# The head of the two MLPs of a decoder trunk: two weight pairs in step, operand sums on VectorE

## The chip, the cores and the metric

One core of a Trainium2 chip runs the whole kernel. The metric is device time in microseconds (us); of the kernel before, three runs took 2951.81, 2952.86 and 2962.06 us, the median is 2952.86 us. The engines have short names in the profile: PE is TensorE (matmul), PEld its weight loads, DVE is VectorE, ACT is ScalarE, POOL is GpSimd, SP is SyncE, which here issues all DMAs.

## The reference, cut to what matters

The trunk has two layers on 1040 tokens (16 meta tokens and 1024 of the input) with a model width of 1024. Each layer is attention with an output projection, and then an MLP with a squared ReLU:

```python
def rms_norm(x, g):
    y = xf * lax.rsqrt(jnp.mean(xf * xf, axis=-1, keepdims=True) + EPS)
    return y * g
def sq_relu_mlp(x, w1, w2):
    h = jax.nn.relu(x @ w1)
    return (h * h) @ w2
# per layer: h = h + attention(...) @ w_out ;  h = h + sq_relu_mlp(rms_norm(h, mlp_norm[i]), w1, w2)
```

w1 is 1024 x 4096 and w2 is 4096 x 1024. The attention parts are the same in both kernels and are not told here.

## The kernel before, in words

Everything is float32. A matrix operand is split into a high half, rounded to the matmul's short form, and a low half, the rest (`split`, L146: a copy on ScalarE, L141, and a subtract on VectorE, L148). A product takes three matmuls: high by high, high by low, low by high.

`mlp` (L902) does one layer's projection and MLP. Tokens are cut into two halves of H (520 in the first layer, 512 in the second), and both MLP matrices are multiplied by Winograd's form of Strassen's scheme: 2x2 blocks and seven products in place of eight. The blocks of the normed activations are x11 and x12 (half 0, channels 0 to 3 and 4 to 7 of 128) and x21 and x22 (half 1). The seven activation operands are A11 = x11, A12 = x12, S1 = x21 + x22, S2 = S1 - x11, S3 = x11 - x21, S4 = x12 - S2 and A22 = x22. A "pair" is 256 columns of the weights; 16 pairs make up w1 and 16 make up w2 (four for each block of 1024 rows), so a layer has 32 pairs of 7 products. A product (L994) is 24 matmuls of 128x260 in the first layer and 12 of 128x512 in the second. Its weight operand is b11, b12, b21, b22 or a sum of these (`w_sum` on GpSimd, L991), split in `w_op` (L965) into one of five buffers.

The order written in the code is: `project_out` (L818) multiplies the attention output by its weights, half 0 and then half 1, eight output tiles of 128 channels each. After each tile `out_evac` (L829) adds the result to the residual h and sums up the squares. `rnorm` (L845) makes 1/rms of a half in y; `normed` (L808) writes x11, x12 and their splits while half 1 is still being projected. After `rnorm(1)` comes the preparation (L936 to L955): for each of the four channel pairs j it makes x21 and x22 on VectorE, four sums on GpSimd and five splits. The pair loop starts at L1032. Its products use three PSUM accumulators: a (A11, S2, S3, A22 into the same one, read out in between), c (S1, then S4) and b (A12). The order is A11, S1, S2, then S4 of the pair before, S3, A12, A22. In w1's pairs the results are squared (`rsq`, or two activations), combined on GpSimd and stored in DRAM (`out`, L1006) in operand form; in w2's pairs they are added into h (`add`, L1014). When four pairs of a block are done, `refresh` (L1018) reads the next block's seven operands back from DRAM in 14 loads (L1027) through two buffers, and splits each.

Each engine runs its own list in order. The lists are drawn up when the kernel is built, by a scheduler that follows the written order as a priority and moves an instruction up where its estimate says that the engine would stand idle. Buffers that share a tag are reused when their last reader is done.

## Time and profile before

| | |
|---|---|
| median of three runs | 2952.86 us |
| the profiled execution, its span | 2952.59 us, 2950.8 us |
| busy: PE, DVE, ACT, POOL | 92%, 71%, 50%, 44% of the span |
| first layer: last projection matmul, first MLP product | 800.7 us, 804.2 us |
| second layer: last projection matmul, first MLP product | 2248.4 us, 2251.7 us |
| chain that ended last, by engine | PE 55%, DVE 21%, DMA 7%, POOL 6%, ACT 6%, issue 5% |

A row of the page or of the trace names the line, the engine and the operation, out<-in by the program's names without buffer numbers (`opa` holds A11 and A12, `opb` S1 and S2, `opc` S3, S4 and A22; `g` is a split weight operand, `t` a weight sum, `ac` a PSUM accumulator, `q` a squared result, `ld` a load buffer of `refresh`). In square brackets stands how long the engine had been idle and what ended that. Times count from the start of the span.

### The profile page before, as it was taken

Reading aid. Unit: us, or ns where it says so; the run is one execution under the profiler, and the core shown is the slowest. Engines: PE = TensorE matmul, PEld = TensorE weight load, DVE = VectorE, ACT = ScalarE, POOL = GpSimd, SP = SyncE. Lnnn points to the kernel's source line nnn. Section 1 sums busy time; section 2 is a strip of 40 time slices with the busy share of each in tenths; the row PEclk is TensorE's granted clock in tenths of the full one; section 3 lists DMA queues with packets and bytes.
Section 4 is the critical chain, followed back from the end, with each engine's and each line's share of the span. In section 5 each row is a group of like instructions: output and inputs, shape, how many; then the busy total and the mean of one; then the engine's idle time right before and its main releaser. Section 6 shows DMA issues by size and latency. Waiting matters only on the chain.

```text
span 2950.8 us, 45897 instructions
## 1 busy us (share of the span) xinstructions
PE 2708.3 (92%) x16698; PEld 2387.9 (81%) x16698; DVE 2092.0 (71%) x3826; ACT 1486.4 (50%) x2828; POOL 1311.3 (44%) x1210
## 2 busy tenths in 40 slices
PE   6889788999979999999988999999997999989999
PEld 6779655677969999999988888889775688867777
DVE  7999989684575456766766888888757655577774
ACT  5777577775333334333434666666743333333332
POOL 2356345431365555322334555555515555543231
PEclk9999779999979999999999999999998999999999
DMA  5312100002314445444411111111312344454442
GB/s 169 80 46 70 49 22 1 1 1 87 93 62 158 146 149 176 143 129 146 158 65 56 51 51 51 52 51 52 105 58 68 121 158 150 153 186 150 150 135 72
DMA packets 243154, 281.93 MB, mean 96 GB/s; under 512 B 22272, under 2 KB 183872, under 8 KB 242928
## 3 DMA queue, kind: packets, MB, share of 16 engines
q1 hardware_dynamic: 242928, 279.01, 30.7%
q8 instruction: 131, 2.15, 0.3%
q14 instruction: 95, 0.78, 0.1%
HBM read 192.42 MB, written 67.63 MB: 88 GB/s over the span
## 4 chain that ended last, share of the span: by engine, by line
PE 55%; DVE 21%; DMA 7%; POOL 6%; ACT 6%; issue 5%; SPq 0%; DVEq 0%; ACTq 0%; POOLq 0%
PE ac L999 32%; PE ps L186 6%; DMA ld<-rdr 5%; PE ps L199 5%; DVE sc L481 3%; PE ps L675 2%; PE ps L733 1%; PE ps L761 1%; PE ps L1322 1%; DVE sc L465 1%; POOL bp L1304 1%; PE ps L758 1%; PE ps L1344 1%; DVE g L148 1%; DVE opa L148 1%
## 5 line engine op out<-in xcount | busy, mean ns | idle before, releaser
L999 PE MATMUL ac<-opc,g 128*128 128x260 f32 (+1 forms) x3456 | 580.0, 324 | 33.5 <-ACT q L141 11.0
L999 PEld LDWEIGHTS ac<-opc,g 128*128 128x128 f32 x3456 | 504.9, 191 | 92.4 <-issue 14.2
L999 PE MATMUL ac<-opb,g 128*128 128x260 f32 (+1 forms) x2304 | 390.2, 325 | 50.8 <-ACT opb L141 35.2
L999 PEld LDWEIGHTS ac<-opb,g 128*128 128x128 f32 x2304 | 336.9, 191 | 94.6 <-ACT opb L141 41.0
L999 PE MATMUL ac<-opa,g 128*128 128x260 f32 (+1 forms) x2304 | 394.5, 324 | 1.6 <-ACT g L141 0.8
L999 PEld LDWEIGHTS ac<-opa,g 128*128 128x128 f32 x2304 | 340.5, 192 | 37.7 <-ACT g L141 1.1
L991 POOL TENSOR_TENSOR t<-rb,t 128x512 f32<-128x512 f32 x128 | 191.8, 1498 | 338.0 <-DMA rb<-in_mlp_w_dram 278.1
L148 DVE TENSOR_TENSOR g<-t,g 128x512 fp32r<-128x512 f32 x256 | 227.6, 889 | 133.5 <-ACT g L141 131.1
L141 ACT ACTIVATE g<-t 128x512 fp32r<-128x512 f32 x256 | 161.1, 629 | 264.2 <-PE ac L999 161.8
L199 PE MATMUL ps<-xhb,wh 128*128 128x256 f32 (+5 forms) x640 | 205.1, 320 | 5.9 <-DVE z L1151 2.7
L199 PE MATMUL ps<-xhb,wl 128*128 128x256 f32 (+5 forms) x640 | 196.8, 307 | 0.0
L199 PE MATMUL ps<-xlb,wh 128*128 128x256 f32 (+5 forms) x640 | 196.3, 307 | 0.0
L991 POOL TENSOR_TENSOR t<-ra 128x512 f32<-128x512 f32 x64 | 95.3, 1489 | 177.4 <-DVE g L148 172.2
L1304 POOL TENSOR_SCALAR bp<-bp,bnm 128x400 f32<-128x400 f32 (+7 forms) x128 | 106.4, 842 | 143.5 <-DVE bnm L1302 143.3
L148 DVE TENSOR_TENSOR g<-rb,g 128x512 fp32r<-128x512 f32 x128 | 113.4, 886 | 57.0 <-ACT g L141 56.9
L675 PE MATMUL ps<-ks,qs 128*128 128x512 f32 (+4 forms) x448 | 131.0, 395 | 21.1 <-DVE qs L606 13.7
L141 ACT ACTIVATE q<-ac 128x520 f32<-128x520 f32 (+1 forms) x96 | 57.7, 601 | 164.4 <-PE ac L999 162.0
L1344 PE MATMUL ps<-bth,bvs 128*128 128x512 f32 (+1 forms) x420 | 135.4, 396 | 3.9 <-DVE qb L1351 2.2
L141 ACT ACTIVATE bth<-ps 128x512 fp32r<-128x512 f32 (+3 forms) x224 | 111.5, 502 | 52.5 <-PE ps L1322 46.5
L199 PEld LDWEIGHTS ps<-xhb,wh 128*128 128x128 f32 x640 | 122.0, 191 | 17.3 <-DVE kr L292 5.1
L148 DVE TENSOR_TENSOR bth<-ps,bth 128x512 fp32r<-128x512 f32 (+3 forms) x210 | 119.6, 571 | 23.0 <-ACT bth L141 21.9
L141 ACT ACTIVATE wh<-wr 128x1024 fp32r<-128x1024 f32 (+1 forms) x84 | 87.3, 1039 | 96.3 <-PE ps L186 71.5
(364 smaller groups left out, 6702.1 us busy)
## 6 DMA issues: line engine op xcount, KB each, us to landing
ra<-in_mlp_w_dram SPq DMA_DIRECT2D x64, 512.0 KB, 3.9
rb<-in_mlp_w_dram SPq DMA_DIRECT2D x64, 512.0 KB, 4.2
ld<-rdr SPq DMA_DIRECT2D x56, 520.0 KB, 4.0
ld<-rdr SPq DMA_DIRECT2D x56, 512.0 KB, 4.3
rdr<-q SPq DMA_DIRECT2D x64, 260.0 KB, 2.1
rdr<-q SPq DMA_DIRECT2D x64, 256.0 KB, 2.2
rdr<-qs SPq DMA_DIRECT2D x48, 260.0 KB, 2.0
wr<-in_a_w_in_dram SPq DMA_DIRECT2D x24, 512.0 KB, 4.1
```

The lines of the kernel that those rows point to most:

```text
L141: nc.scalar.activation(dst, src, AF.Copy, scale=scale)
L148: (nc.gpsimd if pool else nc.vector).tensor_tensor(lo, src, f32(hi), OP.subtract)
L186: nc.tensor.matmul(o[0:n, 0:m], a[:, k, 0:n], b[:, k, s:s + m], start=(k == 0 and j == 0), stop=(k == NK - 1 and j == 2))
L199: nc.tensor.matmul(o[0:n, 0:m], a[:, k, 0:n], b[:, k, s:s + m], start=(k == 0 and j == 0), stop=(k == NK - 1 and j == 2))
L465: nc.vector.scalar_tensor_tensor(sb[:, s:s + m], tm[:, 0:m], wsg[:, b, h:h + 1], sb[:, s:s + m], OP.mult, OP.add)
L481: nc.vector.tensor_scalar(eqb[:, 0:L[b]], scs(b), th, None, op, OP.add, accum_out=dst[:, b:b + 1])
L675: nc.tensor.matmul(o, qs[:, h, :], kc, start=(v == 0), stop=(v == 1))
L733: nc.tensor.transpose(pt[:, j * n:j * n + n], pr[j][:, c0:c0 + P], ident)
L991: nc.gpsimd.tensor_tensor(t, a, c, OP.subtract)
L999: nc.tensor.matmul(t[:, i, 0:m], a[:, j, :], c[:, j, o:o + m], start=start and j == 0 and v == 0, stop=stop and j == 3 and v == 2, skip_gr ...
L1304: nc.gpsimd.tensor_scalar(pr[i], pr[i], nm[:, 3, i:i + 1], 0.0, OP.mult, OP.add)
L1344: nc.tensor.matmul(po[:, j0 * P:], v_kb, th[0:rows, v, j0 * P:], start=(kb == 0 and v == 0), stop=(kb == last and v == 1))
```

## The change

- `out_evac`, in half 1, also sums h times the norm's gain over the two channels of a pair into `st[2]`: a scaled copy on ScalarE for tiles 0 to 3, a multiply-add on VectorE for tiles 4 to 7.
- The preparation is cut up by operand. S1 is that sum times y; S2 = S1 - x11 and S4 = x12 - S2 are made in place; S3 is x22 - S2, with x22 made from h, gain and y. All of it is on VectorE, four channels at a time.
- Pairs 0 and 1 go in step: A11 and A12 of pair 0, then of pair 1; S1 is prepared, and its product is taken for both pairs; then S2 and S4, with both products for both pairs; then S3 and A22. Their weight sums are on VectorE.
- From pair 2 on a pair's order is A11, S1, S2, A12, S4, S3, A22, with S4 within its own pair. S3 and A22 follow one another on accumulator a.
- Accumulators are taken from a list of four that are free, in order of release. `refresh` has three load buffers in place of two; weight sums have three in place of four. The first layer's input tiles for the residual use `st[2]`.

The diff, cut (the removed loop and preparation are in the listing above):

```diff
@@ normed
-                dst = st[j][:, i, 0:H]
+                dst = st[i][:, j, 0:H]
...
@@ out_evac
+                    if half:
+                        us = st[2][:, mi % 4, 0:H]
+                        if mi < 4:
+                            copy(us, sl, gain[:, mi:mi + 1])
+                        else:
+                            nc.vector.scalar_tensor_tensor(us, sl, gain[:, mi:mi + 1], us, OP.mult, OP.add)
...
@@ project_out, x_transposed
-                resid(op)
+                resid(st[2].rearrange("p a b -> p (a b)"))
...
-            xt = op.tile([P, D], F32, tag="xt2", name=f"xt2{t}", bufs=2)
+            xt = spare[:, t % 2 * D:t % 2 * D + D]
...
@@ mlp
-            st = [sp.tile([P, 2, HMAX], F32, name=f"st{layer}{j}") for j in range(4)]
+            st = [sp.tile([P, 4, HMAX], F32, tag=f"st{layer}{j}", name=f"st{layer}{j}") for j in range(3)]
...
+                free, tag_of = [0, 1, 2, 3], {}
                 def accum():
                     n_acc[0] += 1
-                    return pm_.tile([P, 2, 512], F32, tag="acc", name=f"ac{layer}_{n_acc[0]}")
+                    t = pm_.tile([P, 2, 512], F32, tag=f"acc{free[0]}", name=f"ac{layer}_{n_acc[0]}")
+                    tag_of[id(t)] = t, free.pop(0)
+                    return t
+
+                def done(t):
+                    free.append(tag_of.pop(id(t))[1])
+                    return t
...
...
+
+                def prepare(*os):
+                    for o in os:
+                        for j in range(4):
+                            x1, x2, u = (st[i][:, j, 0:H] for i in range(3))
+                            if o == S1:
+                                nc.vector.tensor_tensor(u, u, y[:, b:b + H], OP.mult)
+                                src = u
+                            elif o == S2:
+                                nc.vector.tensor_tensor(x1, u, x1, OP.subtract)
+                                src = x1
+                            elif o == S4:
+                                nc.vector.tensor_tensor(x2, x2, x1, OP.subtract)
+                                src = x2
+                            elif o == S3:
+                                nc.vector.scalar_tensor_tensor(u, h[:, j + 4, b:b + H], gain[:, j + 4:j + 5], y[:, b:b + H],
+                                                               OP.mult, OP.mult)
+                                nc.vector.tensor_tensor(x1, u, x1, OP.subtract)
+                                src = x1
+                            else:
+                                src = u
+                            split(ops[o][0][:, j], ops[o][1][:, j], src)
                 q11 = ep.tile([P, 2, HMAX], F32, tag="sq", name=f"q11_{layer}")
-                q12 = sp.tile([P, 2, HMAX], F32, tag=f"st{layer}0", name=f"q12_{layer}")
-                q2 = sp.tile([P, 2, HMAX], F32, tag=f"st{layer}1", name=f"q2_{layer}")
-                qs = ep.tile([P, 2, HMAX], F32, tag="acc", name=f"qs_{layer}")
+                late = {}
...
-                    t = mp.tile([P, 4, P], F32, tag="wt", name=f"t{layer}_{n}_{i}", bufs=4)
-                    nc.gpsimd.tensor_tensor(t, a, c, OP.subtract)
+                    t = mp.tile([P, 4, P], F32, tag="wt", name=f"t{layer}_{n}_{i}", bufs=3)
+                    (nc.vector if n < 2 else nc.gpsimd).tensor_tensor(t, a, c, OP.subtract)
...
-                        ld = sp.tile([P, 2, HMAX], F32, tag=f"st{layer}{2 + i % 2}", name=f"ld{layer}_{i}")[:, :, 0:H]
+                        if "ld" not in late:
+                            late["ld"] = sp.tile([P, 4, HMAX], F32, tag=f"st{layer}2", name=f"ld{layer}")
+                        g, o2 = ((late["ld"], 0), (late["ld"], 2), (late["c"], 2))[i % 3]
+                        ld = g[:, o2:o2 + 2, 0:H]
...
@@ mlp: the new pair(n) and the new loop; the old loop is in the listing above, L1032 to L1112
+                def pair(n):
+                    b11, b12, b21, b22 = raws.pop(n)
                     up, e = n < NPAIR, n % 2
+                    u1 = q11[:, e, 0:H]
+                    a, t = accum(), {}
+
+                    def q(i):
+                        if "q" not in late:
+                            late["q"] = sp.tile([P, 4, HMAX], F32, tag=f"st{layer}1", name=f"q_{layer}")
+                            late["qs"] = ep.tile([P, 2, HMAX], F32, tag="acc", name=f"qs_{layer}")
+                        return late["q"][:, 2 * i + e, 0:H]
+
+                    def p1():
                         product(a, w_op(b11), ops[A11], True, False)
                         refresh(n, A11)
                         if up:
                             copy(sv(u1), pv(a))
                         else:
                             add(hq(n, 0, 0), a)
+
+                    def p2():
+                        b = accum()
+                        product(b, w_op(b21), ops[A12], True, True)
+                        refresh(n, A12)
+                        if up:
+                            add(sv(u1), b)
+                            rsq(u1)
+                            out(n, A11, u1)
+                        else:
+                            add(hq(n, 0, 0), b)
+                        done(b)
+
+                    def p5():
+                        t[1] = w_sum(n, 1, b12, b11)
+                        t["c"] = c = accum()
+                        product(c, w_op(t[1]), ops[S1], True, False)
                         refresh(n, S1)
+                        t[2] = w_sum(n, 2, b22, t[1])
+
+                    def p6():
+                        c = t["c"]
+                        product(a, w_op(t[2]), ops[S2], False, False)
                         refresh(n, S2)
                         if up:
+                            copy(sv(q(1)), pv(c))
+                            copy(sv(q(0)), pv(a))
                         else:
+                            add(hq(n, 1, 1), c)
                             add(hq(n, 0, 1), a)
+
+                    def p3():
+                        c, u2 = t["c"], q(0)
+                        product(c, w_op(b22), ops[S4], False, True)
+                        refresh(n, S4)
+                        if up:
+                            add(sv(u2), c)
+                            rsq(u2)
+                            out(n, A12, u2)
                         else:
+                            add(hq(n, 0, 1), c)
+                        done(c)
+
+                    def p7():
+                        t[3] = w_sum(n, 3, b22, b12)
+                        product(a, w_op(t[3]), ops[S3], False, False)
+                        refresh(n, S3)
+                        if up:
+                            u3 = q(1)
+                            add(sv(u3), a)
+                            rsq(u3)
+                            out(n, A22, u3)
+                        else:
+                            add(hq(n, 1, 1), a)
+
+                    def p4():
+                        t[4] = w_sum(n, 4, b21, t[2])
+                        product(a, w_op(t[4]), ops[A22], False, True)
+                        refresh(n, A22)
+                        if up:
+                            u2, u3 = q(0), q(1)
+                            s1, s2 = (late["qs"][:, i, 0:H] for i in range(2))
+                            if "c" not in late:
+                                late["c"] = sp.tile([P, 4, HMAX], F32, tag=f"st{layer}0", name=f"c_{layer}")
+                            c21 = late["c"][:, e, 0:H]
+                            nc.scalar.activation(sv(c21), pv(a), AF.Relu)
+                            nc.scalar.activation(c21, c21, AF.Square)
+                            nc.gpsimd.tensor_tensor(s1, c21, u3, OP.add)
+                            out(n, S1, s1)
+                            nc.gpsimd.tensor_tensor(c21, u1, c21, OP.subtract)
+                            out(n, S3, c21)
+                            nc.gpsimd.tensor_tensor(s2, s1, u1, OP.subtract)
+                            out(n, S2, s2)
+                            nc.gpsimd.tensor_tensor(u2, u2, s2, OP.subtract)
+                            out(n, S4, u2)
+                        else:
+                            add(hq(n, 1, 0), a)
+                        done(a)
+                    return p1, p2, p5, p6, p3, p7, p4
+                w_raw(0)
+                w_raw(1)
+                one = pair(0)
+                one[0]()
+                one[1]()
+                two = pair(1)
+                two[0]()
+                two[1]()
+                t2 = op_tile(ep, "xl", f"opb{layer}", 2)
+                t3 = op_tile(mp, "op3", f"opc{layer}", 3)
+                ops.update({S1: view(t2, 0), S2: view(t2, 1), S3: view(t3, 0), S4: view(t3, 1), A22: view(t3, 2)})
+
+                for i, os in enumerate(((S1,), (S2, S4), (), (S3, A22), ())):
+                    prepare(*os)
+                    one[2 + i]()
+                    two[2 + i]()
+                    if i == 3:
+                        w_raw(2)
+                for n in range(2, 2 * NPAIR):
                     if n + 1 < 2 * NPAIR:
                         w_raw(n + 1)
+                    p1, p2, p5, p6, p3, p7, p4 = pair(n)
+                    for p in (p1, p5, p6, p2, p3, p7, p4):
+                        p()
+                    if n >= 2 * NPAIR - 4:
+                        for i in range(2):
+                            after(mp, lambda: done(accum()), 2 * (n % 4) + i)
```

## Rows read from the trace of the kernel before

**Rows 1.** The page's parts 1 and 6, busy time of two engines, one DMA issue.
```profile
PE 2708.3 (92%) x16698; PEld 2387.9 (81%) x16698; DVE 2092.0 (71%) x3826; ACT 1486.4 (50%) x2828; POOL 1311.3 (44%) x1210
...
ra<-in_mlp_w_dram SPq DMA_DIRECT2D x64, 512.0 KB, 3.9
```

**Rows 2.** Stretches: us, busy us (instructions) by engine, granted clock, DMA share, GB/s.
```profile
720.00:800.00 80.00, 78.65 (x647) 77.87 (x646) 38.38 (x61) 29.46 (x43) 19.64 (x11) 1.00 0.30 87
...
804.20:861.50 57.30, 33.14 (x152) 28.34 (x151) 47.64 (x45) 20.77 (x37) 36.35 (x24) 0.64 0.13 41
861.50:1142.80 281.30, 281.30 (x2346) 281.30 (x2347) 141.17 (x184) 96.47 (x167) 160.98 (x112) 1.00 0.44 148
1142.80:1201.60 58.80, 50.73 (x386) 49.87 (x385) 45.63 (x45) 27.12 (x37) 30.23 (x17) 0.91 0.71 221
...
1237.00:1278.00 41.00, 37.44 (x309) 36.90 (x307) 34.68 (x37) 19.78 (x25) 14.33 (x8) 1.00 0.62 191
...
2251.74:2307.69 55.95, 30.42 (x75) 18.80 (x73) 45.99 (x41) 19.66 (x33) 36.86 (x24) 0.66 0.13 42
2307.69:2580.00 272.31, 272.31 (x1183) 221.59 (x1182) 150.52 (x184) 97.53 (x170) 160.60 (x112) 1.00 0.45 152
2580.00:2637.00 57.00, 47.66 (x186) 37.11 (x185) 41.87 (x44) 25.94 (x36) 27.13 (x18) 0.91 0.71 223
...
2674.00:2716.00 42.00, 39.76 (x170) 31.29 (x169) 37.58 (x41) 21.04 (x27) 14.37 (x8) 1.00 0.60 197
```

**Rows 3.** The chain of waits from 800 to 865 us, its shares by line.
```profile
by line: PE ac L999 19.7%; DVE x L942 13.6%; DVE opc L148 10.3%; DVE opb L148 9.9%; DVE g L148 9.4%; issue 8.9%; POOL s L947 4.4%; DVE osqa L856 3.9%; DVE rn L250 3.3%; DVE q L1004 2.6%; POOL x L952 2.5%; POOL s L950 2.0%; ACT opb L141 2.0%
```

**Rows 4.** TensorE in order of time, first MLP's head: start, us, form, count, [idle before].
```profile
804.21 3.24 PE L999 MATMUL ac<-opa,g 128*128 128x260 f32 x24
816.21 0.80 PE L999 MATMUL ac<-opb,g 128*128 128x260 f32 x2 [8.75 <-ACT opb L141]
816.81 1.29 PE L999 MATMUL ac<-opa,g 128*128 128x260 f32 x5
819.48 1.24 PE L999 MATMUL ac<-opb,g 128*128 128x260 f32 x4 [1.39 <-DVE opb L148]
```

**Rows 5.** VectorE in order of time: half 0's norm, half 1's norm, then operand splits.
```profile
757.29 0.43 DVE L856 TENSOR_TENSOR osqa<-rn 128x260 f32<-128x260 f32 x1 [1.95 <-ACT rn L855]
...
759.26 0.43 DVE L250 SCALAR_TENSOR_TENSOR rn<-osqa,rn 128x260 f32<-128x260 f32 x1
...
805.43 2.55 DVE L856 TENSOR_TENSOR osqa<-rn 128x260 f32<-128x260 f32 x2 [1.86 <-ACT rn L855]
...
808.57 2.22 DVE L250 SCALAR_TENSOR_TENSOR rn<-osqa,rn 128x260 f32<-128x260 f32 x2
...
817.67 1.76 DVE L148 TENSOR_TENSOR opb<-s,opb 128x520 fp32r<-128x520 f32 x1
...
829.75 0.69 DVE L148 TENSOR_TENSOR opc<-x,opc 128x520 fp32r<-128x520 f32 x1
830.36 0.69 DVE L148 TENSOR_TENSOR opb<-s,opb 128x520 fp32r<-128x520 f32 x1
```

**Rows 6.** GpSimd beside it, in order of time.
```profile
817.15 1.72 POOL L991 TENSOR_TENSOR t<-rb,ra 128x512 f32<-128x512 f32 x1
```

**Rows 7.** TensorE, then VectorE, then TensorE again: a product's end, its sum, waits on such sums.
```profile
1213.30 3.04 PE L999 MATMUL ac<-opc,g 128*128 128x260 f32 x24
1216.17 3.04 PE L999 MATMUL ac<-opa,g 128*128 128x260 f32 x24
...
1216.37 0.70 DVE L1014 TENSOR_TENSOR ht<-ht,ac 128x520 f32<-128x520 f32 x1 [1.51 <-PE ac L999]
...
1354.91 3.10 PE L999 MATMUL ac<-opc,g 128*128 128x260 f32 x24 [0.92 <-DVE ht L1014]
```

**Rows 8.** SyncE in order of time, the third reload of the first MLP.
```profile
1325.19 6.22 SPq L1027 DMA_DIRECT2D ld<-rdr  x3
...
1368.23 0.32 SPq L1027 DMA_DIRECT2D ld<-rdr  x1
```

More of the change, by code (lines that the diff above doesn't have):

```diff
@@ L929, in sv @@
                     return a.rearrange("p (c m) -> p c m", c=NP)
-                t2 = op_tile(ep, "xl", f"opb{layer}", 2)
-                t3 = op_tile(mp, "op3", f"opc{layer}", 3)
-                ops.update({S1: view(t2, 0), S2: view(t2, 1), S3: view(t3, 0), S4: view(t3, 1), A22: view(t3, 2)})
                 b = s0 + H
-                for j in range(4):
-                    x2 = mp.tile([P, 2, HMAX], F32, tag="x2", name=f"x2_{layer}{j}")
-                    s1 = mp.tile([P, HMAX], F32, tag="s1", name=f"s1_{layer}{j}")[:, 0:H]
-                    x11, x12, x21, x22 = st[j][:, 0, 0:H], st[j][:, 1, 0:H], x2[:, 0, 0:H], x2[:, 1, 0:H]
-                    for x_, k in ((x21, j), (x22, j + 4)):
-                        nc.vector.scalar_tensor_tensor(x_, h[:, k, b:b + H], gain[:, k:k + 1], y[:, b:b + H],
-                                                       OP.mult, OP.mult)
-                    def put(o, src):
-                        split(ops[o][0][:, j], ops[o][1][:, j], src)
-                    nc.gpsimd.tensor_tensor(s1, x21, x22, OP.add)
-                    put(A22, x22)
-                    put(S1, s1)
-                    nc.gpsimd.tensor_tensor(s1, s1, x11, OP.subtract)
-                    put(S2, s1)
-                    nc.gpsimd.tensor_tensor(x21, x11, x21, OP.subtract)
-                    put(S3, x21)
-                    nc.gpsimd.tensor_tensor(x12, x12, s1, OP.subtract)
-                    put(S4, x12)
@@ L1079, in mlp @@
-                    if up:
-                        copy(sv(u3), pv(a))
-                        add(sv(u3), c)
-                        rsq(u3)
-                        out(n, A22, u3)
-                    else:
-                        add(hq(n, 1, 1), a)
-                        add(hq(n, 1, 1), c)
-                    b = accum()
-                    product(b, w_op(b21), ops[A12], True, True)
-                    refresh(n, A12)
-                    if up:
-                        add(sv(u1), b)
-                        rsq(u1)
-                        out(n, A11, u1)
-                    else:
-                        add(hq(n, 0, 0), b)
```

53 lines of the change are left out of this document (2 added, 51 removed).

## The prediction

> **What bounds the kernel now.** I read the page's busy shares first [rows 1]: TensorE is busy 92% of the span, so only the stretches where it waits can give anything. The view of stretches finds them [rows 2]. In the pair loop of the first MLP TensorE is busy for the whole 281.30 us, 2346 matmuls, so 0.1199 us each; in the second it is 272.31 us for 1183, 0.2302 us each. By that pace a pair's 7 products take 7 x 24 x 0.1199 = 20.1 us, and 19.3 us in the second MLP.
>
> The reader is to see two kinds of holes. The heads: the 57.30 us from 804.2 hold 152 matmuls, worth 18.2 us, so 39.1 us are lost; the second MLP's 55.95 us hold 75, worth 17.3 us, so 38.7 us are lost. The granted clock there is 0.64 and 0.66 of the full 2.4 GHz, against 1.00 in the loop; what the slower matmuls cost is in these losses. The reloads of operands: 58.80 us hold 386 matmuls (46.3 us, 12.5 lost) and 41.00 us hold 309 (37.0 us, 4.0 lost); in the second MLP 14.2 and 2.9 us are lost. Taking the first of three later reloads in each layer for all three, the eight lose 12.5 + 14.2 + 3 x 4.0 + 3 x 2.9, about 47 us.
>
> Then the chain of waits through the first head [rows 3]: matmuls are 20% of it; the rest of the named lines is nearly all VectorE, with one GpSimd sum. TensorE in order of time [rows 4] shows the first product (A11) at 804.21, and then 8.75 us of waiting for the first piece of S1. It also shows that the engine's list leaves the written order: matmuls of S1 alternate with `opa` ones, which the code writes after S2, and it still waits in between. VectorE in order of time [rows 5] shows the price of company: the six half-size operations of the norm take from 757.29 to 759.68, 2.4 us, for half 0, and from 805.43 to 810.79, 5.4 us, for half 1; an operand's subtract takes 1.76 us beside a GpSimd sum [rows 6], and 0.69 us alone, with 0.61 us from one to the next.
>
> **The change, part by part.** The head first. Before, 14 products' worth of matmuls (336, 40.3 us) would be done at 804.2 + 40.3 + 39.1 = 883.6. After it, A11 and A12 of two pairs (4 products, 11.5 us) need nothing from half 1, so TensorE can run from 804.2 to 815.7. S1 needs one VectorE operation per channel, as its sum is there already. The GpSimd sums are gone from this stretch, so I price VectorE at the uncontended step of 0.61 us. It has, from 805.4 on: the norm 2.4 us; 20 operations that make operands (4 for S1, 4 for S2, 4 for S4, 8 for S3); 20 low halves of operands; 12 low halves of weights (14 products, the two b11 done before); 6 weight sums (8, the two S1 ones in the idle time before 805.43); 12 sums and squares of results (two for each of three products and two pairs). That is 70 x 0.61 + 2.4 = 45.1 us. Never idle, it would end at 850.5, and with the last product (2.9 us) the head ends at 853.4. At the busy share of the old head, 47.64 of 57.30 us or 0.83, it takes 54.3 us, and the head ends at 862.6. I take the middle, 858.0, as nothing says how well the new list is packed: a gain of 25.6 us. Bounds: TensorE without a wait, 844.5 (39 us gained), and the case that VectorE is the bound (14 us, below). The second head has the same instructions with 512 elements in place of 520 and loses 38.7 us now: 25 us. Together 51 us.
>
> The Trainium skill, page "Perfetto Trace Analysis", section "Optimizing Scalar/DVE Operations", speaks against this part: if VectorE is saturated, work may better go to another engine, GpSimd among them, while it warns that the two share a read port. The rows show both sides: VectorE is busy 83% of the old head, and it is slowed to more than twice its time by GpSimd. By the first half of the advice the gain would be that of the rival "VectorE bounds the head"; by the second, mine.
>
> The sum during the projection adds, per layer, 4 scaled copies on ScalarE and 4 multiply-adds on VectorE. Both lie under the projection's matmuls: TensorE is busy 78.65 of 80 us there, VectorE 38.38 and ScalarE 29.46 [rows 2]. The last multiply-add falls into the 1.86 us in which VectorE is idle before the norm [rows 5]. I cost it at nothing; without that cover it is 0.7 us a layer.
>
> Raw weights: pairs 0 and 1 hold both buffers, so pair 2's first load can start only when S3's weight sums are made, and takes 3.9 us to land [rows 1]. VectorE then still has A22's splits to do, so I take nothing; bound 4 us a layer. On SyncE's queue both loads of pair 1 now stand ahead of the first stores, which nothing reads until the first reload. The input tiles in `st[2]`, the free list of accumulators, three weight-sum buffers: nothing, because each is released a whole product or more ahead of its next use; bounds 3 us either way.
>
> From pair 2 on there is a new wait. S3 and A22 use accumulator a one after the other, and VectorE has to read a in between; before, A12 stood there. Sixty pairs have this. When a product ends, the next one starts at 1216.17, and the sum of the ended one starts 0.20 us later and takes 0.70 us; a product that had to wait for such a sum stood still for 0.92 us [rows 7]. Queued behind the waiting matmul are A22's others and the whole next pair. But the next pair's A11 has a free accumulator and split weights, and the list can put its matmuls there, as it did in rows 4. I take 0.15 us a pair, for the list's estimate being a little short: near the filled end, since A11 is ready by four products. That is +9 us; bounds 0 and 60 x 0.92 = 55 us, and more if something stands before the sum.
>
> The reloads get a third buffer and lose a slack: S4's operand was needed a pair later, and now 14 loads have to be there within the pair. In the third reload 14 loads are issued from 1325.19 to 1368.23, 3.3 us apart with two buffers [rows 8]. Counted from A11's start at the reload, A22 of the next pair begins 13 x 2.88 = 37.4 us later. With two loads ahead and ten to come at 3.3 us, plus some 5 us until the first buffer is free (A11's product, 2.9 us, and a split) and 2 us for a split (an estimate: three subtracts of 0.69 us, as a load is twice the size and is copied too), the old order is ready at 40, 3 us late, which is what the later reloads lose. With three buffers and eleven to come, it is ready at 43 us if the pace stays, and at 31 if three buffers give 2.2 us. With DMA engines already busy 0.62 to 0.71 of the time there [rows 2] I take a pace between, 2.8 us: 38 us, about on time, which would save some 15 us in the later six; against that the first reload of each layer, with stores running beside it, may lose more. I take -5 us; bounds -47 (all of the loss) and +16 (pace unchanged).
>
> Sum, against the profiled execution's 2952.6 us: -51 + 9 - 5 = -47, so 2906 us. The median of the three runs is 0.3 us higher than that execution, so nothing has to be converted.
>
> **The rivals.**
> "VectorE bounds the head": its list gets all the work of the stretch, at whole durations of 0.69 us and a busy share of 0.83: 70 x 0.69 + 2.4 = 50.7, over 0.83 is 61.1 us, so the head ends at 869.4 and gains 14 us; 28 for both, 2929 us. For it: VectorE has been the chain. Against: GpSimd's company, which made its time, is gone.
>
> "The reload's pace doesn't change": +16 in place of -5, 2927 us. For it: the DMA share. Against: between issues SyncE waits for a free buffer.
>
> "The accumulator's wait stays open": the list doesn't fill it, 55 in place of 9 us: 2952 us, nothing gained. For it: in rows 4 the list left holes. Against: those were holes with no operand ready.
>
> "The wait stays open and is longer", the other side: VectorE's list has one weight subtract (0.69 us) ahead of the sum, 0.92 + 0.69 = 1.61 us a pair, 97 us: 2994 us, slower. It decides from (51 + 5) / 60 = 0.93 us a pair on, which eats the gain, and from 1.18 us on the kernel is slower by 0.5%.
>
> That the change doesn't do what it says, the head's order being drawn up differently, is a part of the first rival.
>
> **How the numbers follow.** My forecast, 2906 us, has a chance of 0.57 and a range of its own of 2885 to 2930. VectorE as bound 0.13; the reload's pace 0.07, of it 0.02 together with the former, at 2950; the open wait 0.10; the longer one 0.13. About 0.5% (15 us) is what can be told from no change: faster 0.75, same 0.12, slower 0.13. The range goes from 2876 (heads gain 29 each, reloads 22, the wait costs 4) to 2953, and leaves out the longer wait, a little of the open one and a little below.
>
> **What would show it.** In the profile after: 336 matmuls from the first MLP product in about 54 us, not 79.6; no GpSimd sum of operands there, VectorE's subtracts at 0.69 us, the granted clock of the head above 0.64. In the loop a pair still every 20.1 us, with A11 matmuls of the next pair between S3 and A22, and hardly any TensorE idle time put down to L1014's counterpart. Wrong: a TensorE idle of 0.9 us or more in every pair, or a head of 65 us.

## The result, and the profile after

The changed kernel takes 2916.35 us (median of four runs, 2905.59 to 2922.37), the kernel before, beside it, 2952.34 us: a ratio of 0.9878, 95% interval 0.9854 to 0.9901. The profiled execution of after is the slowest of its four, 2922.37 us with a span of 2920.6 us, against 2950.8 us before.

The code up to the first MLP is nearly the same everywhere, yet the first product started between 796 and 809 us in the profiles of this study. So times are compared by stretches. I took them from TensorE in order of time, counting matmuls: products 1 to 14 (the head), 15 to 105 (13 pairs without a reload), 106 to 224 (the rest, where the reloads are). A cell is good to about 1 us, and each is from one execution: where kernels of this study have the same code in a stretch, their cells differ by up to 3 us, in the last column by 5 (late_sum of experiment 4 has 368.2 there). Smaller differences say nothing by themselves. "Between" runs from the first MLP's last product to the second's first.

| us | head 1 | 15-105 | 106-224 | between | head 2 | 15-105 | 106-224 |
|---|---|---|---|---|---|---|---|
| before | 79.7 | 261.8 | 369.0 | 737.0 | 78.3 | 251.7 | 361.1 |
| after | 54.1 | 265.2 | 373.2 | 727.7 | 55.9 | 257.6 | 372.4 |

The heads give 48 us, the stretch between 9.3; the loops take back 9.3 and the stretches with reloads 15.5; the first product came 1.7 us later. The sum is -30.8, and the spans differ by 30.2.

The page of after, parts 1 and 6, answering to [rows 1]:
```profile
PE 2697.7 (92%) x16698; PEld 2383.4 (82%) x16698; DVE 2048.8 (70%) x3874; ACT 1489.8 (51%) x2836; POOL 1248.2 (43%) x1162
...
ra<-in_mlp_w_dram SPq DMA_DIRECT2D x64, 512.0 KB, 4.0
...
ld<-rdr SPq DMA_DIRECT2D x38, 520.0 KB, 4.6
```
Stretches of after, columns as in [rows 2]: both heads, a piece of loop, the first reload.
```profile
805.86:859.95 54.09, 44.52 (x339) 43.49 (x337) 49.65 (x81) 27.21 (x48) 5.73 (x5) 0.94 0.24 76
2226.09:2281.94 55.85, 44.42 (x170) 34.45 (x169) 50.24 (x79) 26.75 (x46) 5.97 (x5) 0.91 0.23 74
900.00:1140.00 240.00, 240.00 (x1997) 239.39 (x1996) 113.02 (x153) 84.38 (x145) 145.78 (x95) 1.00 0.42 146
1140.00:1200.00 60.00, 49.01 (x377) 48.57 (x376) 43.51 (x47) 22.58 (x30) 25.16 (x15) 0.89 0.61 201
```
The same 14 products in the kernel before (the second window ends about 1 us before the 14th product does):
```profile
804.20:883.80 79.60, 55.44 (x338) 50.64 (x337) 59.69 (x60) 28.70 (x50) 49.00 (x33) 0.74 0.21 69
2251.74:2329.10 77.36, 51.83 (x167) 36.03 (x166) 58.05 (x57) 28.19 (x48) 48.62 (x32) 0.76 0.19 64
```
In the new head VectorE does 81 instructions in 49.65 us, 0.61 us each; in the old one 60 in 59.69, 0.99 each. GpSimd's busy time fell from 49.00 to 5.73 us, and the granted clock rose from 0.74 to 0.94.

VectorE in order of time in after's head: half 1's norm [rows 5], then S1 and its splits.
```profile
807.07 0.77 DVE L862 TENSOR_TENSOR osqa<-rn 128x260 f32<-128x260 f32 x2 [0.91 <-ACT rn L861]
...
809.11 1.28 DVE L148 TENSOR_TENSOR g<-rb,g 128x512 fp32r<-128x512 f32 x2
810.31 1.92 DVE L953 TENSOR_TENSOR st<-st,rn 128x520 f32<-128x520 f32 x3
812.14 1.92 DVE L148 TENSOR_TENSOR opb<-st,opb 128x520 fp32r<-128x520 f32 x3
```
The norm is over after 2.1 us, where it took 5.4.

TensorE in after's first head, answering to [rows 4]:
```profile
805.86 3.71 PE L1010 MATMUL ac<-opa,g 128*128 128x260 f32 x28
809.85 8.39 PE L1010 MATMUL ac<-opa,g 128*128 128x260 f32 x68 [0.28 <-DVE g L148]
...
830.54 6.44 PE L1010 MATMUL ac<-opb,g 128*128 128x260 f32 x40 [4.99 <-DVE g L148]
...
846.66 13.45 PE L1010 MATMUL ac<-opc,g 128*128 128x260 f32 x96 [3.94 <-ACT g L141]
```
The four early products run on end where the old head waited 8.75 us. What are left are two holes. The first is at a weight split that is queued behind VectorE's operand splits, the second at ScalarE's copy of a weight sum that VectorE makes at 845.26, also behind operand splits.

TensorE in after's loop, one pair:
```profile
939.73 0.52 PE L1010 MATMUL ac<-opc,g 128*128 128x260 f32 x3
940.09 1.11 PE L1010 MATMUL ac<-opa,g 128*128 128x260 f32 x8
941.04 3.14 PE L1010 MATMUL ac<-opc,g 128*128 128x260 f32 x24
944.02 2.09 PE L1010 MATMUL ac<-opa,g 128*128 128x260 f32 x16
```
Between S3 (the `opc` product that ends at 940) and A22 (at 941.04) stand 8 matmuls of the next pair's A11, which then finishes with 16. The pair takes 20.2 us.

At the first reload, TensorE and then VectorE:
```profile
1145.12 0.40 PE L1010 MATMUL ac<-opb,g 128*128 128x260 f32 x2
1153.07 5.28 PE L1010 MATMUL ac<-opc,g 128*128 128x260 f32 x24 [7.54 <-DVE q L1025]
```
```profile
1149.50 1.23 DVE L148 TENSOR_TENSOR opa<-ld,opa 128x1040 fp32r<-128x1040 f32 x1
1150.65 1.75 DVE L1015 SCALAR_TENSOR_TENSOR q<-q 128x520 f32<-128x520 f32 x1
1152.33 0.68 DVE L1025 TENSOR_TENSOR q<-q,ac 128x520 f32<-128x520 f32 x1
```
A22 waits 7.54 us for the sum at 1152.33, which reads its accumulator; ahead of that sum VectorE's list has the splits of reloaded operands. The same at a later reload of the second MLP (`c` in these rows is the third load buffer):
```profile
2736.55 3.04 PE L1010 MATMUL ac<-opc,g 128*128 128x512 f32 x12 [3.28 <-DVE h L1025]
```
```profile
2731.56 1.22 DVE L148 TENSOR_TENSOR opa<-ld,opa 128x1024 fp32r<-128x1024 f32 x1
2732.70 0.68 DVE L148 TENSOR_TENSOR g<-t,g 128x512 fp32r<-128x512 f32 x1
2734.09 1.80 DVE L148 TENSOR_TENSOR opa<-c,opa 128x1024 fp32r<-128x1024 f32 x1 [0.71 <-ACT opa L141]
2735.82 0.68 DVE L1025 TENSOR_TENSOR h<-h,ac 128x512 f32<-128x512 f32 x1
```
Over the span, the products' waits for such sums add up to 47.2 us in after (19.8 for `q`, 14.6 for `h`, 12.8 for `ht`), where they were 19.4 before (14.1 for `ht`, 5.3 for `h`). Before, products waited another 11.0 us for ScalarE's copies out of an accumulator, in after 2.0: for read-outs of either kind it is 49.2 us against 30.4.

### The profile page after: what moved, and what is told of

Read it like the earlier page. It is cut to its first block, busy times and chain, and to the rows that moved or that the text cites. A ratio compares the mean times of both kernels' runs of the same rounds, so it can differ in the third digit from the quotient of the medians.

```text
span 2920.6 us, 45848 instructions
## 1 busy us (share of the span) xinstructions
PE 2697.7 (92%) x16698; PEld 2383.4 (82%) x16698; DVE 2048.8 (70%) x3874; ACT 1489.8 (51%) x2836; POOL 1248.2 (43%) x1162
## 4 chain that ended last, share of the span: by engine, by line
PE 59%; DVE 22%; DMA 5%; POOL 5%; issue 5%; ACT 5%; SPq 0%; DVEq 0%; ACTq 0%; POOLq 0%
PE ac L1010 34%; PE ps L186 6%; PE ps L199 6%; DVE sc L481 3%; DMA ld<-rdr 2%; PE ps L675 2%; PE ps L1402 2%; PE ps L1380 1%; PE ps L733 1%; PE ps L758 1%; PE ps L761 1%; DVE g L148 1%; PE ps L1348 1%; POOL bp L1362 1%; DVE sc L465 1%
## 5 line engine op out<-in xcount | busy, mean ns | idle before, releaser
L1010 PE MATMUL ac<-opc,g 128*128 128x260 f32 (+1 forms) x3456 | 586.9, 328 | 51.3 <-DVE q L1025 16.2
L1010 PE MATMUL ac<-opb,g 128*128 128x260 f32 (+1 forms) x2304 | 377.3, 321 | 15.1 <-DVE g L148 7.6
L1002 POOL TENSOR_TENSOR t<-rb,t 128x512 f32<-128x512 f32 x120 | 175.4, 1461 | 397.8 <-DVE g L148 252.9
L148 DVE TENSOR_TENSOR g<-t,g 128x512 fp32r<-128x512 f32 x256 | 204.4, 803 | 99.0 <-ACT g L141 95.4
L141 ACT ACTIVATE g<-rb 128x512 fp32r<-128x512 f32 x128 | 80.2, 628 | 204.6 <-PE ac L1010 202.4
L148 DVE TENSOR_TENSOR g<-rb,g 128x512 fp32r<-128x512 f32 x128 | 102.7, 806 | 72.8 <-ACT g L141 72.6
L1025 DVE TENSOR_TENSOR h<-h,ac 128x512 f32<-128x512 f32 x112 | 76.3, 684 | 107.7 <-PE ac L1010 107.7
L1025 DVE TENSOR_TENSOR ht<-ht,ac 128x520 f32<-128x520 f32 x112 | 77.5, 692 | 90.0 <-PE ac L1010 89.8
```

The source lines that it names most:

```text
L141: nc.scalar.activation(dst, src, AF.Copy, scale=scale)
L148: (nc.gpsimd if pool else nc.vector).tensor_tensor(lo, src, f32(hi), OP.subtract)
L1002: (nc.vector if n < 2 else nc.gpsimd).tensor_tensor(t, a, c, OP.subtract)
L1010: nc.tensor.matmul(t[:, i, 0:m], a[:, j, :], c[:, j, o:o + m], start=start and j == 0 and v == 0, stop=stop and j == 3 and v == 2, skip_gr ...
L1025: nc.vector.tensor_tensor(dst, dst, pv(t), OP.add)
```

## The experiments

Orders of the loop and places of S4 (experiments 1, 6 and 7, and s4_late_b2 in 8) have four runs each; sums_pool, one_pair, late_sum, two_bufs and the two kernels without reloads have one.

**1. Which order of the loop?** Three products of a pair change places in the loop of after.
```diff
-                    for p in (p1, p5, p6, p2, p3, p7, p4):   # after: A11 S1 S2 A12 S4 S3 A22
+                    for p in (p1, p5, p6, p2, p7, p3, p4):   # order_s4: S4 between S3 and A22
+                    for p in (p1, p5, p6, p3, p7, p2, p4):   # order_a12: A12 there, as before
```


> The changed kernel with one edit: from pair 2 on the order is A11, S1, S2, A12, S3, S4, A22, so S4's product stands between the two that share accumulator a. Theory (the changed kernel's lost part is the wait for the sum that reads a between S3 and A22: 0.07 us a pair in the first MLP and 0.23 us in the second, and up to 7.5 us at a reload, where that sum stands behind reload splits in VectorE's list): a pair goes back to 20.15 and 19.36 us, the waits of 7.5 and 6.9 us at the first reloads go, 9 us from the loops and 10 to 20 us from the reloads, so about 2892 us, ratio to the kernel before 0.980. Rival (the reload is limited by the loads' pace, and the wait only moves to the next product that lacks its operand): only the loops' 9 us, about 2907 us, ratio 0.985.

> The changed kernel with the order A11, S1, S2, S4, S3, A12, A22 from pair 2 on: A12 stands between S3 and A22 as in the kernel before. Theory: the same relief on accumulator a as with S4 in between, but A12's operand buffer is free two products later at the end of the first MLP, and the next stage's input, which uses that buffer, is split later: the 8 us that the changed kernel gained between the MLPs are lost again. About 2900 us, ratio 0.983, and 5 us or more of TensorE idle time at the end of the first MLP. Rival (that gain between the MLPs comes from how the list fell out, not from A12's place): the same time as with S4 in between, and no such idle time.

order_s4 took 2915.1 us (ratio to before 0.9872, 0.9847 to 0.9897), order_a12 2913.87 us (0.9875, 0.9851 to 0.9899): both the same as after.

| us | head 1 | 15-105 | 106-224 | between | head 2 | 15-105 | 106-224 |
|---|---|---|---|---|---|---|---|
| order_s4 | 55.3 | 262.5 | 374.3 | 729.5 | 54.6 | 254.4 | 370.8 |
| order_a12 | 54.2 | 262.2 | 378.6 | 731.0 | 54.9 | 254.4 | 372.8 |

In the loop without reloads a product between S3 and A22 gives 2.7 and 3.2 us, a part of it in the loop's first pair: the accumulator's wait was real there, and small. With reloads nothing is gained, and the long wait stays, in order_s4 at the product after S3:
```profile
1143.97 2.32 PE L1010 MATMUL ac<-opc,g 128*128 128x260 f32 x9 [6.87 <-DVE q L1025]
```
So the theory that S3 next to A22 makes the reload slow fell. The stretch between is 3.3 us longer in order_a12 than in after, where the theory had 8; TensorE's waits at the start of the next stage are 0.20, 1.46 and 1.48 us, not 5.

**2. The sums on GpSimd.** The activation sums and the first pairs' weight sums go back to GpSimd, order and buffers of after.
```diff
-                                nc.vector.tensor_tensor(u, u, y[:, b:b + H], OP.mult)
+                                nc.gpsimd.tensor_tensor(u, u, y[:, b:b + H], OP.mult)
...
-                    (nc.vector if n < 2 else nc.gpsimd).tensor_tensor(t, a, c, OP.subtract)
+                    nc.gpsimd.tensor_tensor(t, a, c, OP.subtract)
```


> The changed kernel with the sums of the preparation and all weight sums on GpSimd, the rest as it is, the two pairs in step and the early sum too. Theory (GpSimd's company doubles VectorE's times in the head, and that is what the move bought): 336 matmuls from the first MLP product take 68 to 76 us in place of 54.1, VectorE's subtracts show 1.2 us or more on average. Rival (the four products that need nothing from half 1, and pairs in step, bring the gain; where the sums run is of no matter): 54 to 60 us.

It took 2940.03 us; the heads 66.8 and 65.8 us, some 13 and 10 more than after's and a little under the theory's 68 to 76.
```profile
806.17:872.90 66.73, 47.46 (x337) 46.54 (x337) 59.40 (x59) 27.16 (x48) 45.99 (x29) 0.82 0.23 72
```
```profile
814.42 6.94 DVE L148 TENSOR_TENSOR opb<-st,opb 128x520 fp32r<-128x520 f32 x4
```
VectorE has 22 instructions fewer and is busy 10 us longer: four operand splits take 6.94 us beside GpSimd, where after's three take 1.92. The two heads together lose about half of what they had gained; that price takes in VectorE's slower operations and the time of the sums on GpSimd, which this run doesn't take apart. The page "Perfetto Trace Analysis" of the Trainium skill, section "Optimizing Scalar/DVE Operations", which the prediction weighed, says that work of a saturated VectorE may go to GpSimd, and warns that this might not help, as the two share a read port. The trace agrees with the warning, by the 6.94 us above; that the port is the reason, no run here shows.

**3. One pair in the head.** Pair 0 alone goes through the preparation; pair 1 is an ordinary pair of the loop.
```diff
-                two = pair(1)
-                two[0]()
-                two[1]()
...
-                for n in range(2, 2 * NPAIR):
+                for n in range(1, 2 * NPAIR):
```


> The changed kernel with pair 0 alone in the head (A11, A12, S1, S2, S4, S3, A22 with the preparation in between), and pair 1 as the loop's first. Theory (VectorE's list of some 45 us is the bound of the head, and the build's scheduler moves pair 1's ready products into the holes by itself): 336 matmuls from the first MLP product take 56 to 62 us. Rival (the written order of two pairs in step matters): 66 to 75 us, with holes of 5 us and more before S2 and S3.

It took 2926.5 us; the heads 62.1 and 60.9 us. Going in step is worth 8 and 5 us. The times lie at the upper end of the theory's 56 to 62; holes of 5 us and more were the rival's sign, and they are there. They are the same two as in after, but longer, with less work ahead of them:
```profile
822.65 4.70 PE L1010 MATMUL ac<-opb,g 128*128 128x260 f32 x20 [6.21 <-DVE g L148]
...
837.35 1.24 PE L1010 MATMUL ac<-opc,g 128*128 128x260 f32 x4 [6.96 <-ACT g L141]
```

**4. S1's channel sum written after the projection.**
```diff
-                    if half:
+                    if False:
...
+                                nc.vector.tensor_scalar(u, h[:, j, b:b + H], gain[:, j:j + 1], None, OP.mult)
+                                nc.vector.scalar_tensor_tensor(u, h[:, j + 4, b:b + H], gain[:, j + 4:j + 5], u, OP.mult, OP.add)
```


> The changed kernel with the channel sum of S1 made after the projection, by eight more operations on VectorE in each head (four of about 0.4 us, four of 0.69 us). Theory, VectorE is the engine that the head waits for: each head's 14 products take 4.4 us more, 58.7 and 60 us. Rival, the extra operations lie beside A12 and cost nothing: 54 and 55.5 us.

It took 2918.67 us; heads 54.4 and 55.8 us, as in after. But this doesn't price a late sum, for the scheduler moved the operations up into the projection by itself (VectorE, the first and the last of the eight):
```profile
779.12 2.33 DVE L953 TENSOR_SCALAR st<-ht,ng 128x520 f32<-128x520 f32 x3
...
804.90 0.76 DVE L954 SCALAR_TENSOR_TENSOR st<-ht,ng,st 128x520 f32<-128x520 f32 x1
```
In after the last one starts at 804.81. What is shown is that neither the place where the sum is written nor ScalarE's part in it matters to the head.

**5. No reloads.** In both kernels, so each computes the second product with the first's operands.
```diff
+                    return
                     for hh in range(2):
```


> The changed kernel without the reloads: the transfers that bring the second product's operands back from DRAM and their splits are left out, so it computes the second half of each MLP with the first half's operands. Theory, reloads cost the changed kernel some 15 us more than the kernel before (63 against 49 in both MLPs): near 2857 us. Rival, the reloads cost both kernels the same and the loss lies in the loop: near 2872 us, or 30 us below the run beside it.

> The kernel before the change without the reloads (left out in the same way). Theory: near 2903 us, so that the difference to the changed kernel without reloads is some 46 us, which is heads, loop and joins alone (47 - 9 + 8). Rival: 2903 us as well, but a difference of 30 us, as with reloads.

They took 2858.77 and 2904.57 us, both within 2 us of the theory.

| us | head 1 | 15-105 | 106-224 | between | head 2 | 15-105 | 106-224 |
|---|---|---|---|---|---|---|---|
| before_norel | 79.8 | 261.6 | 342.6 | 734.0 | 79.1 | 251.6 | 336.6 |
| after_norel | 55.3 | 267.0 | 345.2 | 726.8 | 56.1 | 256.1 | 339.6 |

The reloads cost 369.0 - 342.6 = 26.4 and 361.1 - 336.6 = 24.5 us before, 28.0 and 32.8 after: 10 us more, 8 of them in the second MLP. The rest of the loss, 15.5 us (5.4 + 4.5 + 2.6 + 3.0), is in the loops and has nothing to do with reloads. 7 us of the difference of the two times is the earlier start (802.2 against 809.3), so that this difference, 45.8 us, meets the theory's 46 is luck: without the start it is 39.

**6. S4 one pair late again.** From pair 2 on; the diff is cut. In s4_late the late S4 stands between S3 and A22, in s4_late_b where it stood before the change.
```diff
-                    for p in (p1, p5, p6, p2, p3, p7, p4):
+                    for p in (p1, p5, p6, p2, p7, None, p4):   # s4_late; None: S4 of pair n-1, then w_raw(n+1)
+                    for p in (p1, p5, p6, None, p7, p2, p4):   # s4_late_b
```


> The changed kernel with S4 put back one pair late from pair 2 on, as it stood before the change (the first two pairs keep theirs in place): A11, S1, S2, A12, S3, S4 of the pair before, A22. Theory, the product in place takes a product's length of slack from the reload (six operands reloaded beside seven products before, seven beside seven after) and S3 next to A22 leaves the accumulator's wait open: both come back, from the end of the 14 products to each MLP's last product 631 and 614 us as in the kernel before, pair periods 20.15 and 19.36 us, span near 2897 us (2920.6 less 24). Rival, the reload loss has another cause, such as three transfers in flight or the order of VectorE's list: only the loop's 9 us come back, span near 2911 us, and the long waits of A22 or S4 on the sum that reads the accumulator (7 us) stay at the reloads.

> As the run beside it, but with the whole loop in the order of the kernel before: A11, S1, S2, S4 of the pair before, S3, A12, A22, so that A12 is the sixth product of a pair and not the fourth. Theory of the joins (the early A12 sets its operand's buffer free, which the next stage's splits fill, and that was worth some 8 us): the stretch between the two MLPs is 737 us again and not 728, and the whole is about 8 us slower than the run beside it, near 2905 us. Rival, the joins gained by something else (the head's buffers, the last S4 no longer after the loop): no more than 2 us between the two runs.

s4_late took 2933.12 us (0.9942, 0.9922 to 0.9962), s4_late_b 2901.95 us (0.9836, 0.981 to 0.9863).

| us | head 1 | 15-105 | 106-224 | between | head 2 | 15-105 | 106-224 |
|---|---|---|---|---|---|---|---|
| s4_late | 55.2 | 262.2 | 371.1 | 730.2 | 55.2 | 257.8 | 394.6 |
| s4_late_b | 54.6 | 265.4 | 367.1 | 736.2 | 54.6 | 257.3 | 357.2 |

s4_late_b and order_a12 have one order of products and differ in S4's pair (and in what goes with it: S4's store, and the next weights' load behind it). The late S4, with what goes with it, saves 11.5 and 15.6 us in the stretches with reloads. s4_late's span, 2931.1 us, missed the theory by 34. About 18 us of it are its last two whole pairs, 29.5 and 31.9 us where s4_late_b has 21.9 and 21.6: the load of the next weights is written behind the late S4, and in the last pairs behind the output's stores too, and stands sixth there. In SyncE's order of time that load goes out at 2862.98; ScalarE idles 7.34 us for it, and TensorE 4.28 us for the weight split:
```profile
2855.29 4.81 SPq L1465 DMA_DIRECT2D out_dram<-ot  x2
2862.98 0.38 SPq L997 DMA_DIRECT2D rb<-in_mlp_w_dram  x1
```
```profile
2867.03 0.63 ACT L141 ACTIVATE g<-rb 128x512 fp32r<-128x512 f32 x1 [7.34 <-DMA rb<-in_mlp_w_dram]
```

The stretch between the MLPs is 736.2 us again, as the theory of the joins had it. But order_a12, whose A12 is late too and whose S4 is in place, has 731.0, and s4_late, whose S4 is late and whose A12 is early, has 730.2. So either of the two changes alone brings most of the gain, and neither is shown to be the larger part. In s4_late_b, with both late, the next stage waits 5.02 us for the last S4's additions (first row below); in s4_late that wait is 1.89 us.

**7. The last pair's S4 in place.** s4_late_b, with the last pair in its own order.
```diff
-                    for p in (p1, p5, p6, None, p7, p2, p4):
+                    for p in (p1, p5, p6, None, p7, p2, p4) if n < 2 * NPAIR - 1 else (p1, p5, p6, None, p2, p7, p3, p4):
```


> The run with S4 one pair late and the old order of the loop (2901.95 us), with the last pair alone in another order: A11, S1, S2, S4 of the pair before, A12, S3, its own S4, A22. Theory of the joins (5.02 us of idle time at the end of the first MLP are the last S4's additions, which the next stage's splits wait for, and a few more us go in the lower clock behind that idle time): the idle time goes, the stretch between the two MLPs is 728 to 731 us instead of 736.2, the whole near 2895 us. Rival, the early A12 inside all pairs or the changed buffers make the difference: still near 736 us and 2902 us.

It took 2899.99 us (0.9815, 0.9796 to 0.9835), the fastest of the study; its interval ends below after's (0.9854 to 0.9901). Against s4_late_b alone the difference can't be told. The stretch between is 732.4 us, 4 less than 736.2, where the theory had 5 to 8: the wait for the sums is gone, but one of 2.94 us for a weight split has come. TensorE at the join in s4_late_b, then in s4_late_c:
```profile
1492.64 1.18 PE L186 MATMUL ps<-xhb,wh 128*112 128x348 f32 x3 [5.02 <-DVE ht L1025]
```
```profile
1487.42 0.63 PE L186 MATMUL ps<-xhb,wh 128*112 128x348 f32 x3
...
1491.47 0.74 PE L186 MATMUL ps<-xhb,wl 128*112 128x348 f32 x3 [2.94 <-DVE wl L148]
```

**8. Two load buffers or three.** In after (two_bufs) and in s4_late_b (s4_late_b2).
```diff
-                        g, o2 = ((late["ld"], 0), (late["ld"], 2), (late["c"], 2))[i % 3]
+                        g, o2 = ((late["ld"], 0), (late["ld"], 2))[i % 2]
```


> The changed kernel with two load buffers instead of three, S4 in place. Theory, seven reloads in a pair are bound by the order of VectorE's list and not by the buffers: products 106 to 196 at 286 to 290 and 280 to 284 us (285.83 and 280.51 with three). Rival, three transfers in flight are what makes the reload of the changed kernel slow: 283 and 274 us, as in the kernel before.

> S4 one pair late and the old order of the loop, with two load buffers for the reload instead of three. Theory, the third buffer is worth what the prediction gave it (some 5 us in both MLPs): the products 106 to 196 take 283.5 and 273 us, as in the kernel before (283.14 and 273.54), where three buffers took 281.92 and 270.58; the whole near 2906 us. Rival, the third buffer is worth nothing: 282 and 270.6 us again, 2902 us.

| us | head 1 | 15-105 | 106-224 | between | head 2 | 15-105 | 106-224 |
|---|---|---|---|---|---|---|---|
| two_bufs | 54.3 | 264.3 | 384.1 | 727.4 | 53.8 | 258.4 | 370.9 |
| s4_late_b2 | 55.0 | 263.1 | 367.1 | 735.0 | 54.5 | 258.4 | 362.8 |

two_bufs took 2923.0 us, s4_late_b2 2906.21 us (0.9834, 0.9815 to 0.9853). With S4 late the third buffer is worth 0 and 5.6 us, near the prediction's 5, though the ratios of s4_late_b and s4_late_b2 can't be told apart. With S4 in place it is worth 10.9 us in the first MLP and -1.5 in the second. By the products 106 to 196 that the expectation named, two_bufs has 297.2 and 282.3 us: the second fits the theory, the first neither side. Of the differences only the 10.9 is clear of the spread between kernels with the same code. That three transfers in flight make after's reload slow is ruled out, though each takes longer to land: 4.6 us in after (520 KB), 4.1 in two_bufs.

## Why the prediction was right, and where it was not

**The heads, -51 forecast, -48 measured.** The first gained 25.6 (25.6 forecast), the second 22.4 (25): there the last hole is 5.66 us, not 3.94. The price was right, 0.61 us an operation and a norm of 2 us; VectorE had 81 instructions, not 76 (the 70 and six of the norm), and was busy 0.92 of the head, near the 0.91 that the middle between the two cases comes to. Experiment 2 gives about half of the gain to having no sums on GpSimd, experiment 3 a fifth to a third to going in step; what the early channel sum gives was not measured. The rival "VectorE bounds the head", with its busy share of 0.83 and 14 us a head, is out, but VectorE is still what the head's holes wait for. One reading was short: in [rows 3] not one but three lines are GpSimd sums, 8.9% together, which speaks for the change.

**The accumulator's wait, +9 forecast.** The list put A11 matmuls of the next pair between S3 and A22, as the step said. Where nothing else disturbs, a pair takes 20.22 us for 20.15 and 19.59 for 19.36; over 30 pairs each that is 2 + 7 = 9 us. That this meets the forecast is in part luck. In order_a12, with A12 between S3 and A22 as before, a pair takes 20.10 and 19.51 us, so the wait is worth 0.12 and 0.08 us a pair, some 6 us in all; the other 0.15 us a pair in the second MLP is there in every order of experiments 1 and 6, and its cause is open. Both rivals of the open wait are out: from 900 to 1140 us TensorE never stands still. The sign "hardly any idle time put down to the sums", though, was wrong: at the reloads they hold up TensorE.

**Raw weights of pair 2, 0 forecast, bound 4 us a layer.** The first pair of the loop took 22.4 us for 20.1 and 21.8 for 19.4, so some 5 us in all, within the bound. But no product there waits for a weight operand. TensorE's idle time in the first MLP's pair is 1.07 us, for a ScalarE copy out of an accumulator, and 0.77 us, for a sum:
```profile
866.92 3.14 PE L1010 MATMUL ac<-opb,g 128*128 128x260 f32 x24 [1.07 <-ACT q L141]
...
880.39 3.14 PE L1010 MATMUL ac<-opc,g 128*128 128x260 f32 x24 [0.77 <-DVE q L1025]
```
The copy, at 866.27, had waited 4.47 us for GpSimd's sums of the pair before. Ahead of these GpSimd has the first weight sums, which wait for those loads:
```profile
851.29 1.44 POOL L1002 TENSOR_TENSOR t<-ra 128x512 f32<-128x512 f32 x1 [50.21 <-DMA ra<-in_mlp_w_dram]
855.58 1.29 POOL L1002 TENSOR_TENSOR t<-rb,t 128x512 f32<-128x512 f32 x1 [2.85 <-DMA rb<-in_mlp_w_dram]
```
So the late weights can have cost the 1.07 us, by way of GpSimd's list; that they cost the 5 is not shown.

**The reloads, -5 forecast, +10 measured: the step that failed.** It set S4's lost slack against a third buffer and let the buffer win. Measured by themselves, the late S4, with its store and the weights' load that go with it, is worth 27 us in these stretches (experiment 6, with three buffers), and the third buffer about 5 with S4 late and 9 with S4 in place (both MLPs together). By pair times the first reload of each layer costs about 15 us in after (12.6 and 14.5 before), the other six together 32 (24 before), where my step let the other six gain. It counted the loads against a deadline, with one split behind the last. What it left out is that all fourteen splits (1.2 us and more each) stand in VectorE's list, ahead of sums for which products wait. The size came near the rival "The reload's pace doesn't change" (+16 in place of -5), and its mechanism, the pace of the transfers, isn't out. At both reloads shown above VectorE's list itself had stood still for a copy that waited for a load. VectorE, then ScalarE twice:
```profile
1141.94 1.24 DVE L148 TENSOR_TENSOR opb<-ld,opb 128x1040 fp32r<-128x1040 f32 x1 [2.66 <-ACT opb L141]
...
1140.83 1.07 ACT L141 ACTIVATE opb<-ld 128x1040 fp32r<-128x1040 f32 x1 [5.87 <-DMA ld<-rdr]
...
2733.01 1.06 ACT L141 ACTIVATE opa<-c 128x1024 fp32r<-128x1024 f32 x1 [1.10 <-DMA c<-rdr]
```
In the stretches with reloads ScalarE's copies of operands waited 97 us for loads in after (168 before), and VectorE 42 us for such copies (67 before). How much of the loss is the order of the list, and how much the loads that it waits for, no experiment takes apart.

**Between the MLPs, nothing forecast, -9.3 measured.** No step of the prediction looked there, so that it made up for most of the reloads' loss is luck. TensorE at the end of the first MLP, in the kernel before and in after:
```profile
1519.58 0.92 PE L186 MATMUL ps<-xhb,wh 128*112 128x346 f32 x2 [4.72 <-DVE ht L1014]
1520.30 1.07 PE L186 MATMUL ps<-xlb,wh 128*112 128x348 f32 x3
```
```profile
1498.25 0.63 PE L186 MATMUL ps<-xhb,wh 128*112 128x348 f32 x3
1498.72 0.63 PE L186 MATMUL ps<-xlb,wh 128*112 128x348 f32 x3
```
With S4 in place the additions to the residual are done earlier, and the 4.72 us go. With that idle time goes a slow start too: three matmuls took 1.07 us behind it, at a granted clock of 0.50 (1.2 GHz) from 1519.6 to 1525.0, and 0.63 us in after, at 1.00. Experiments 1, 6 and 7 show the parts: 737.0 with S4 late and A12 late, 731.0 with A12 late alone, 730.2 with S4 late alone, 727.7 with neither. Here S4 in place helps, at the reloads it hurts; s4_late_c takes both sides.

By these terms: -48 + 9 + 5 + 10 - 9.3, and 1.7 for the later start, is -31.6, where the stretches sum up to -30.8. So the forecast of 2906 us was 10 us too good against the median and 16 against the profiled execution; the reloads alone made 15 of it, the first pairs 5 and the heads 3, and the join gave 9 back. What stays open: why the reloads of the second MLP lost more in after (8 us) than those of the first (2); some of it can be the spread of 5 us in that stretch.

## What to carry to other kernels

When a step is moved to an earlier deadline, count it on every engine that it passes: the reload was priced by its transfers and one split, and its fourteen splits, some of them waiting for a load, stood ahead of other work on VectorE. Two placements of one step can be right in two places of a loop; where a product holds a shared buffer or closes a stage, its place in the last iteration is a choice of its own. And an experiment that moves work in the written order shows nothing until the trace shows that it moved.

## What the runs showed of the hardware

VectorE with GpSimd at work beside it was slowed to more than twice its time for plain subtracts: 6.94 us for four of 128x520 (sums_pool) where three took 1.92 with GpSimd idle (after), 1.73 against 0.64 us each, in a kernel that changed nothing but the engine of the sums.

An idle time of 4.7 to 5.0 us on TensorE was followed by matmuls at 0.36 us apiece (1.07 for three) in place of 0.21, for some 5 us, in two kernels (before and s4_late_b). The stretches of before, busy up to 1514.8, then idle, then slow, then fast again:
```profile
1508.00:1514.80 6.80, 6.80 (x57) 6.59 (x56) 5.98 (x6) 5.81 (x7) 1.93 (x2) 1.00 0.42 129
1514.80:1519.50 4.70, 0.06 (x1) 0.00 (x0) 4.70 (x4) 1.99 (x3) 3.27 (x3) 0.90 0.10 38
1519.60:1525.00 5.40, 5.40 (x19) 5.40 (x20) 5.40 (x3) 2.98 (x3) 3.34 (x1) 0.50 0.24 97
1525.00:1530.00 5.00, 5.00 (x32) 5.00 (x31) 2.50 (x3) 0.00 (x0) 0.00 (x0) 0.96 0.23 58
```
In s4_late_b the clock behind the 5.02 us was 0.50 too, from 1492.7 to 1498.0.
